# Eight of 22 k tiles of an FFN's last product computed as seven block products

## The chip, the cores and the metric

The kernel runs on one core of one Trainium2 chip. The metric is the device time of one execution in microseconds (us), the median of several runs; lower is better. The engines of the core are TensorE (PE, matrix products, with PEld for its weight loads), VectorE (DVE), ScalarE (ACT), GpSimd (POOL) and SyncE (SP). Operands lie in SBUF, matmul results in eight PSUM banks of 512 fp32 columns.

## What is computed

One block of a network for 512 tokens of width 1024, all in fp32: an FFN with half weight, a mixer (short convolution, gated linear attention, two gates), a second FFN with half weight, and a norm. The change concerns the second FFN and the end:

```python
def rmsnorm(x, g):
    y = x * lax.rsqrt(jnp.mean(x * x, axis=-1, keepdims=True) + EPS)
    return y * g

def swiglu(x, w_gu, w_down):
    g, u = jnp.split(x @ w_gu, 2, axis=-1)      # 1024 -> 2 x 2816
    return (jax.nn.silu(g) * u) @ w_down        # 2816 -> 1024

x = x + 0.5 * swiglu(rmsnorm(x, norm_ffn1_g), ffn1_w_gu, ffn1_w_down)
x = x + hybrid_mixer(rmsnorm(x, norm_mix_g), ...)
x = x + 0.5 * swiglu(rmsnorm(x, norm_ffn2_g), ffn2_w_gu, ffn2_w_down)
return rmsnorm(x, final_norm_g)
```

## The kernel before

**Three matmuls for one.** Each fp32 operand is split into a high part in the matmul's own type (fp32r) and a low part, the rest. A product is the sum of high x high, high x low and low x high. ScalarE casts the high part and VectorE subtracts to get the low part: for weights on lines 293 and 294 (`wh`, `wl`, rings of three buffers of 128 x 1024), for the FFN's hidden values on 649 and 650 (`split_hid`), for the operands of the sets below on 533 and 534 (`Operands.make`). The last two write to the pool `op`, 14 buffers of 128 x 1024.

**Weights.** `PLAN` lists the weight units in the order of their use and `STEPS` the steps that use them. `Weights.take` hands out the next split unit and issues the splits of the two steps after it. Raw units are loaded by SP (line 267) into the pool `f`, ten buffers, with 512 KB each. A down projection's unit is one k tile: 128 rows by 1024 columns.

**Sets.** Most of the up projections, and of the mixer's, are done in sets: a product of two by two blocks in seven block products instead of eight (Winograd's form). The names are m1, p2, q6, p5, q7, p4, p3. The weight sums of a set are made by accumulating DMAs on POOL (`Weights.add`, line 271) and one VectorE addition (`s3`, line 280); the operand sums by VectorE in place (`Operands.sum`); they are made once in each stage. A step of a set is 24 matmuls of 256 columns (line 485). `Operands.ORDER` is the order in which the operands are made; the steps themselves come in the order of `order()`.

**The FFN.** `ffn` computes a first group and two pairs of columns plainly (`plain_pair`), then nine sets (`up_set`), each of which leaves two k tiles of the hidden values. These are tiles of the pool `hid` (eleven buffers of 128 x 1024), which also holds the four normed operands at first. During the second FFN's sets `natural` transposes X so that tokens lie on partitions, X being the residual.

**The last product.** For the second FFN `last_down` follows: tokens on the partitions of the result, so the hidden values are the stationary operand and the weights the moving one. For each of 22 k tiles it runs four token tiles x two column halves x three matmuls of 512 columns (lines 700 to 702), into all eight PSUM banks. The last four k tiles (`TAIL`) are different: their weights and hidden values are split ahead, and bank by bank, token tile by token tile, the twelve matmuls that remain for a bank are followed by its evacuation into X (line 726), the final norm and the store, while TensorE goes on with the next bank.

**Who sets the order.** The framework's planner orders the instructions of each engine by its own simulation of the program, with program order as the priority, and places the waits; buffers of a pool are handed out in program order. Only the tail's part is in a fixed order (`manual_schedule`).

Of the kernel before, what the change touches and what calls it, by code (L numbers as in the profile page):

```python
# [12 lines left out]
ALU = mybir.AluOpType  # L13
ENG = mybir.EngineType

P = 128
S = 512
# [45 lines left out]
def full(mat, kt):  # L63
    return [(mat, k, 1, (0,), 1024) for k in range(kt)]
# [42 lines left out]
def units(us):  # L107
    for u in us:
        STEPS.append((len(PLAN), None))
        PLAN.append(u)  # L110
# [12 lines left out]
         ("conv", 3), ("cb", 0), ("cb", 1), ("r", 0), ("r", 1)]  # L123


def ffn_plan(up, down, plain, slow):

    units(group(up, KD, (0, DFF, P, DFF + P), slow))
    for f in range(2, plain):
        units(single(up, KD, f * P))  # L130
        units(single(up, KD, DFF + f * P))
    sets(up, [(s * HW, DFF + s * HW) for s in range(plain // 2, KF // 2)])
    units(full(down, KF))
    ENDS.append(len(STEPS))


# [31 lines left out]
def block_kernel(ctx: ExitStack, tc: tile.TileContext, xT, vecs, gf, gup, wgl, wts, out):  # L168
# [28 lines left out]
    def MM():  # L197
        cnt[0] += 1
        return ps.tile([P, S], F32, tag="mm", name=f"mm{cnt[0]}")
# [27 lines left out]
    class Weights:  # L227
# [3 lines left out]
        def __init__(self, ahead):  # L231
            self.ahead = ahead
            self.issued = 0
            self.taken = 0
            self.end = 0
            self.ready = []
            self.raw = {}
            self.loads = {}
            self.sums = {}

        def phase(self, early, first=6):


            self.early = early
            lo, self.end = self.end, [e for e in ENDS if e > self.end][0]
            for i in range(lo, self.end):
                n, p = STEPS[i]
                if p == "m1":
                    self.loads.setdefault(max(lo, i - first), []).append(n)
                    first = 6  # L250
                    self.sums.setdefault(max(lo + 3, i - 3), []).append(n)
            self.fetch(lo)

        def fetch(self, at):
# [15 lines left out]
        def add(self, out_, a):  # L270
            nc.gpsimd.dma_start(out_, a, accum_op=ALU.add)  # L271

        def issue(self):
            at = self.issued
            self.fetch(at)
            for n in self.loads.get(at, ()):
                self.raw[n] = [self.dma(n + i) for i in range(4)] + [tile_of("f", [P, 1024])]
            for n in self.sums.get(at, ()):
                a11, a12, a21, a22, s3 = self.raw[n]
                nc.vector.tensor_tensor(out=s3, in0=a11, in1=a21, op=ALU.add)  # L280
                self.add(a21, a22)
            n, p = STEPS[at]
            w = unit_cols(PLAN[n])
            if p is None:
                raw = self.raw[n]
            else:
                a11, a12, a21, a22, s3 = self.raw[n]
# [5 lines left out]
            nc.scalar.copy(h[:, :w], raw[:, :w])  # L293
            nc.vector.tensor_tensor(out=l[:, :w], in0=raw[:, :w], in1=h[:, :w].bitcast(F32),  # L294
                                    op=ALU.subtract)
# [162 lines left out]
    def mul(out_, a, b, eng=None):  # L458
        (eng or nc.vector).tensor_tensor(out=out_, in0=a, in1=b, op=ALU.mult)
# [34 lines left out]
    class Operands:  # L494

        ORDER = ("m1", "p2", "p5", "q6", "q7", "p4", "p3")

        def __init__(self, b):  # L500
            self.b = b
# [57 lines left out]
    def ffn(up, down, norm, nxt, plain, at):  # L559
# [6 lines left out]

        o = mm_group(up, KD, (0, DFF, P, DFF + P), xh, xl, extra=finish, slow=nxt is not None)
        row = rows[0]
        xn = {}

        def normed(j, l):

            if (j, l) not in xn:
                t = slice(l * HW, (l + 1) * HW)
                v = tile_of("hid", [P, 1024]).rearrange("p (k t) -> p k t", t=HW)
                for i in range(4):
                    k = 4 * j + i
# [8 lines left out]
        hid = []  # L586

        def plain_pair(f, g, u):
            if f % 2 == 0:
                hid.append(tile_of("hid", [P, 2, S]))  # L590
# [4 lines left out]
            mul(hid[-1][:, f % 2], s, t)  # L595

        xo.make("m1")
        plain_pair(0, o[0], o[1])
# [9 lines left out]
            plain_pair(f, g, u)  # L608

        def up_set(i):  # L610
            h = tile_of("hid", [P, 2, S])
            hid.append(h)

            def done(s, p):
                bank, v = s.bank, s.v
# [29 lines left out]
        def split_hid(k):  # L645

            h, l = (tile_of("op", [P, 2, S], F32R) for _ in range(2))
            t = hid[k // 2]
            nc.scalar.copy(h, t)  # L649
            nc.vector.tensor_tensor(out=l, in0=t, in1=h.bitcast(F32), op=ALU.subtract)  # L650
            return h, l

        us = full(down, KF)
        if nxt is None:
            return last_down(us, split_hid)
        o = [AUX(), AUX()] + [MM() for _ in range(KD - 2)]

        def mm(d, k, w, hl):
# [28 lines left out]
    def last_down(us, split_hid):  # L687
        X = XS[-1]
        gr = []
        for e in range(2):  # L690
# [6 lines left out]
        def mm(t, e, k, w, hl):  # L697
            wh, wl = (a[:, 512 * e : 512 * (e + 1)] for a in w)
            a, b = (v[:, k % 2, t * P : (t + 1) * P] for v in hl)
            nc.tensor.matmul(o[t][e], a, wh, start=k == 0, stop=False)  # L700
            nc.tensor.matmul(o[t][e], a, wl, start=False, stop=False)  # L701
            nc.tensor.matmul(o[t][e], b, wh, start=False, stop=k == KF - 1)  # L702

        for k in range(KF - TAIL):
            if k % 2 == 0:
                hl = split_hid(k)
            w = W.take(us[k])
            for t in range(NTB):
                for e in range(2):
                    mm(t, e, k, w, hl)  # L710
        w = [W.take(u) for u in us[KF - TAIL :]]
        hl = [split_hid(k) for k in range(KF - TAIL, KF, 2)]
        fin = []
        ys = [[] for _ in range(NTB)]

        def blocks(t):
            return t.rearrange("p (d i) -> p d i", i=P)

        last = NTB - 1

# [606 lines left out]
```

## Time and profile before

| | us |
|---|---|
| median of 3 runs | 1212.69 (1212.53 to 1212.84) |
| profiled execution, its own time | 1210.31 |
| span in the profile | 1208.6 |
| PE busy | 1196.6 |
| VectorE busy | 768.5 |
| ScalarE busy | 579.5 |
| granted clock of TensorE, mean | 0.999 |

The second FFN's last product begins at 1081.8 us of the span; its last matmul starts at 1201.3. A row of a timeline gives the start, the duration, the engine, the line, the operation, output and inputs, and in brackets how long the engine had been idle and what ended that. A row of groups gives engine, line, operation, shapes and count, then busy us and mean ns of one, then the idle time ahead of them. Matmuls overlap, so their durations are longer than their spacing.

### The profile page before, as it was taken

The numbers are of one execution on the slowest core, as the hardware profiler recorded it, in microseconds if no ns is written. First come the engines' busy times: TensorE is split into PE (matmuls) and PEld (weight loads), VectorE is DVE, ScalarE is ACT, GpSimd is POOL, SyncE is SP. The second block draws the span as 40 slices with busy tenths as digits, with TensorE's granted clock in tenths as the row PEclk, the third lists the DMA queues.
The fourth block names the chain that finished last, engine by engine and source line by source line (L and its number), as shares of the span: only waits on it lengthen the run. The fifth ranks groups of instructions, "written<-read, shape, count | busy, mean of one in ns | idle before, by whom it ended". The sixth has DMA issues, their size and how long they took to land.

```text
span 1208.6 us, 18730 instructions
## 1 busy us (share of the span) xinstructions
PE 1196.6 (99%) x7738; PEld 1095.3 (91%) x7738; DVE 768.5 (64%) x923; ACT 579.5 (48%) x718; POOL 89.7 (7%) x125
## 2 busy tenths in 40 slices
PE   9999999999999999998999999999999999999997
PEld 8899999988888889998999998888889999998886
DVE  7976666732277765767678685555597656583325
ACT  6554455532254466858554572234356445562323
POOL 0011111000010000010111100100001111100000
PEclk9999999999999999999999999999999999999999
DMA  9477777521162326766767766513347777752201
GB/s 348 98 197 188 179 190 180 174 88 61 53 244 88 89 69 159 205 170 165 186 184 175 191 178 214 200 63 129 113 101 192 186 176 176 182 182 90 70 1 69
DMA packets 55876, 181.33 MB, mean 150 GB/s; under 512 B 6288, under 2 KB 10512, under 8 KB 55792
## 3 DMA queue, kind: packets, MB, share of 16 engines
q1 hardware_dynamic: 36912, 124.27, 29.6%
q0 software_dynamic: 14240, 51.39, 23.0%
q10 hardware_dynamic: 4640, 4.49, 1.1%
q8 instruction: 60, 0.98, 0.3%
q14 instruction: 24, 0.20, 0.0%
HBM read 124.55 MB, written 8.39 MB: 110 GB/s over the span
## 4 chain that ended last, share of the span: by engine, by line
PE 97%; ACT 1%; DVE 1%; issue 0%; DMA 0%; DVEq 0%
PE mm L485 49%; PE mm L322 7%; PE mm L321 7%; PE mm L323 7%; PE mm L345 7%; PE mm L701 2%; PE mm L700 2%; PE mm L702 2%; PE mm L362 1%; PE mm L364 1%; PE mm L363 1%; PE aux L322 1%; PE aux L701 1%; PE aux L321 1%; PE aux L702 1%; PE aux L700 1%
## 5 line engine op out<-in xcount | busy, mean ns | idle before, releaser
L485 PE MATMUL mm<-op,wh 128*128 128x256 f32 x3360 | 608.0, 284 | 0.5 <-ACT wh L293 0.5
L293 ACT CAST wh<-f 128x1024 fp32r<-128x1024 f32 (+1 forms) x307 | 320.6, 1046 | 522.1 <-PE mm L485 205.6
L294 DVE TENSOR_TENSOR wl<-f,wh 128x1024 fp32r<-128x1024 f32 (+1 forms) x307 | 373.4, 1219 | 274.1 <-ACT wh L293 263.3
L485 PEld LDWEIGHTS mm<-op,wh 128*128 128x128 f32 x3360 | 523.8, 191 | 1.6 <-ACT wh L293 0.7
L485 PE MATMUL mm<-op,wl 128*128 128x256 f32 x1680 | 476.6, 284 | 2.5 <-DVE wl L294 2.5
L485 PEld LDWEIGHTS mm<-op,wl 128*128 128x128 f32 x1680 | 321.4, 191 | 2.8 <-DVE wl L294 2.7
L321 PE MATMUL mm<-op,wh 128*128 128x512 f32 x388 | 151.5, 390 | 0.0
L323 PE MATMUL mm<-op,wl 128*128 128x512 f32 x388 | 151.3, 390 | 0.0
L322 PE MATMUL mm<-op,wh 128*128 128x512 f32 x388 | 151.1, 389 | 0.0
L271 POOL DMA_DIRECT2D f<-f x90 | 77.7, 863 | 781.5 <-DVE wl L294 458.9
L323 PEld LDWEIGHTS mm<-op,wl 128*128 128x128 f32 x388 | 72.9, 188 | 15.1
L321 PEld LDWEIGHTS mm<-op,wh 128*128 128x128 f32 x388 | 72.9, 188 | 15.1
L322 PEld LDWEIGHTS mm<-op,wh 128*128 128x128 f32 x388 | 72.9, 188 | 14.9
L345 PE MATMUL mm<-op,wh 128*128 128x512 f32 x256 | 63.5, 390 | 0.2 <-DVE op L396 0.2
L345 PEld LDWEIGHTS mm<-op,wh 128*128 128x128 f32 x256 | 48.0, 188 | 10.5 <-issue 0.3
L490 ACT COPY tp<-mm 128x512 f32<-128x512 f32 x90 | 52.1, 579 | 2.8 <-PE mm L485 2.7
L700 PE MATMUL mm<-wh,op 128*128 128x512 f32 x108 | 42.1, 390 | 0.0
L701 PE MATMUL mm<-wl,op 128*128 128x512 f32 x108 | 42.1, 390 | 0.0
L702 PE MATMUL mm<-wh,op 128*128 128x512 f32 x108 | 42.1, 389 | 0.0
L650 DVE TENSOR_TENSOR op<-hid,op 128x1024 fp32r<-128x1024 f32 x22 | 26.9, 1222 | 17.7 <-ACT op L649 17.7
L280 DVE TENSOR_TENSOR f<-f,f 128x1024 f32<-128x1024 f32 x30 | 36.7, 1224 | 0.8
L345 PE MATMUL mm<-op,wl 128*128 128x512 f32 x128 | 34.3, 390 | 0.0
(247 smaller groups left out, 1113.8 us busy)
## 6 DMA issues: line engine op xcount, KB each, us to landing
f<-wts SPq DMA_DIRECT2D x219, 512.0 KB, 4.1
f<-f POOLq DMA_DIRECT2D x90, 512.0 KB, 4.9
X<-xT SPq DMA_DIRECT2D x8, 256.0 KB, 5.0
xs<-X POOLq DMA_DIRECT2D x8, 256.0 KB, 5.8
ga<-tp ACTq DMA_DIRECT2D x8, 256.0 KB, 2.8
gb<-tp ACTq DMA_DIRECT2D x8, 256.0 KB, 3.9
tp<-ga SPq DMA_DIRECT2D x8, 256.0 KB, 5.9
tp<-gb SPq DMA_DIRECT2D x8, 256.0 KB, 2.6
```

Source lines behind the costliest of these rows:

```text
L271: nc.gpsimd.dma_start(out_, a, accum_op=ALU.add)
L293: nc.scalar.copy(h[:, :w], raw[:, :w])
L294: nc.vector.tensor_tensor(out=l[:, :w], in0=raw[:, :w], in1=h[:, :w].bitcast(F32), op=ALU.subtract)
L321: nc.tensor.matmul(o, wh, ah, start=first, stop=False)
L322: nc.tensor.matmul(o, wh, al, start=False, stop=False)
L323: nc.tensor.matmul(o, wl, ah, start=False, stop=last)
L345: nc.tensor.matmul(o[c], w[:, s : s + P], a[k], start=k == 0 and j == 0, stop=k == kt - 1 and j == 2)
L485: nc.tensor.matmul(to, ww[:, s], aa[:, t], start=fresh and k == 0 and e == 0 and j == 0, stop=k == 3 and j == 2, skip_group_check=True)
L490: nc.scalar.copy(v, o)
L700: nc.tensor.matmul(o[t][e], a, wh, start=k == 0, stop=False)
L701: nc.tensor.matmul(o[t][e], a, wl, start=False, stop=False)
L702: nc.tensor.matmul(o[t][e], b, wh, start=False, stop=k == KF - 1)
```

## The change

- In the last product, the k tiles 8 to 17 come first, as before, each with 24 matmuls into eight banks. They are then closed and added to X with the factor 0.5 (eight VectorE instructions).
- The k tiles 0 to 7 follow as one two-by-two block product: two halves of four k tiles, two halves of 256 tokens, two halves of 512 columns, in seven block products in the order m1, p2, q6, p5, q7, p3, p4. Each takes two weight units (half of its k tiles each) of 128 x 1024 and runs 24 matmuls of 512 columns into two banks. Bank pair b collects m1, q6, q7 and p4, c collects p5 and p3, a holds p2. After each block product the running sum of its bank pair is added to one quarter of X with the factor 0.5 or -0.5, in two VectorE instructions (`uses`).
- The seven operands come from the hidden values through the class `Operands`; six of them are made during the ten direct k tiles, p4 after them. The weight sums are made as for the sets, for two sets of four units at once (`CHUNK_STEP`, `loads`, `sums`).
- The last four k tiles are as before, in new PSUM buffers; their raw weights are loaded at given steps (`pre`).
- The hidden values lie in one tile of 22 k tiles in both FFNs, and the normed operands in its last eight. The pools change: `f` eleven instead of ten, `tp` (scratch) eight instead of nine, `hid` one.
- `Operands.ORDER` has p3 ahead of p4, for all users of the class.

```diff
+CHUNK = 8
+CHUNK_ORDER = ("m1", "p2", "q6", "p5", "q7", "p3", "p4")
+CHUNK_STEP = {}
+
+def last_plan(down):
+    us = full(down, KF)
+    units(us[CHUNK : KF - TAIL])
+    firsts = []
+    for s in range(2):
+        firsts.append(len(PLAN))
+        PLAN.extend((down, 4 * j + 2 * s, 2, (512 * i,), 512) for i in range(2) for j in range(2))
+    CHUNK_STEP.update({(s, p): len(STEPS) + 2 * i + s for i, p in enumerate(CHUNK_ORDER)
+                       for s in range(2)})
+    STEPS.extend((n, p) for p in CHUNK_ORDER for n in firsts)
+    units(us[KF - TAIL :])
...
-    units(full(down, KF))
+    if slow:
+        units(full(down, KF))
+    else:
+        last_plan(down)
...
-                if p == "m1":
+                if p == "m1" and i in CHUNK_STEP.values():
+                    at = CHUNK_STEP[0, "m1"]
+                    self.loads.setdefault(at - (4 if i == at else 2), []).append(n)
+                    self.sums.setdefault(i, []).append(n)
+                elif p == "m1":
...
+            if self.end == len(STEPS):
+                c = CHUNK_STEP
+                for i, at in enumerate((c[0, "q6"], c[1, "q6"], c[1, "p3"], c[1, "p3"])):
+                    self.pre.setdefault(at, []).append(STEPS[self.end - TAIL + i][0])
...
-                self.raw[n] = [self.dma(n + i) for i in range(4)] + [tile_of("f", [P, 1024])]
+                self.raw[n] = [self.dma(n + i) for i in range(4)]
             for n in self.sums.get(at, ()):
+                self.raw[n].append(tile_of("f", [P, 1024]))
...
+            for n in self.pre.get(at, ()):
+                self.raw[n] = self.dma(n)
...
-        ORDER = ("m1", "p2", "p5", "q6", "q7", "p4", "p3")
+        ORDER = ("m1", "p2", "p5", "q6", "q7", "p3", "p4")
...
+        hid = tile_of("hid", [P, KF, S])
...
-                v = tile_of("hid", [P, 1024]).rearrange("p (k t) -> p k t", t=HW)
+                f = KF - KD + 4 * j
+                v = hid[:, f : f + 4, t]
...
-            h = tile_of("hid", [P, 2, S])
-            hid.append(h)
+            h = hid[:, plain + 2 * i : plain + 2 * i + 2]
...
-            nc.tensor.matmul(o[t][e], a, wh, start=k == 0, stop=False)
+            nc.tensor.matmul(o[t][e], a, wh, start=k in (CHUNK, KF - TAIL), stop=False)
             nc.tensor.matmul(o[t][e], a, wl, start=False, stop=False)
-            nc.tensor.matmul(o[t][e], b, wh, start=False, stop=k == KF - 1)
-
-        for k in range(KF - TAIL):
-            if k % 2 == 0:
-                hl = split_hid(k)
+            nc.tensor.matmul(o[t][e], b, wh, start=False, stop=k in (KF - TAIL - 1, KF - 1))
...
+        def add(t, e, bank, by):
+            xt = X[:, 4 * e : 4 * e + 4, t * P : (t + 1) * P]
+            nc.vector.scalar_tensor_tensor(out=xt, in0=blocks(bank), scalar=by, in1=xt,
+                                           op0=ALU.mult, op1=ALU.add)
+
+        ho = Operands(lambda j, l: hid[:, 4 * j : 4 * j + 4, l * HW : (l + 1) * HW])
+        hls = {k: split_hid(k) for k in (CHUNK, CHUNK + 2)}
+        more = [4, 6, 8, "m1", "p2", "p5", "q6", "q7", "p3"]
+        for k in range(CHUNK, KF - TAIL):
             w = W.take(us[k])
             for t in range(NTB):
                 for e in range(2):
-                    mm(t, e, k, w, hl)
+                    mm(t, e, k, w, hls[k - k % 2])
+            if more:
+                n = more.pop(0)
+                if isinstance(n, int):
+                    hls[CHUNK + n] = split_hid(CHUNK + n)
+                else:
+                    ho.make(n)
+        for t in range(NTB):
+            for e in range(2):
+                add(t, e, o[t][e], 0.5)
+        ho.make("p4")
+
+        uses = {"m1": [(0, 0, 0.5)], "p2": [(0, 0, 0.5)], "q6": [(1, 0, 0.5)],
+                "p5": [(1, 1, -0.5)], "q7": [(1, 1, -0.5)], "p3": [(1, 0, 0.5)],
+                "p4": [(0, 1, -0.5)]}
+        banks = {}
+        for p in CHUNK_ORDER:
+            b = {"p2": "a", "p5": "c", "p3": "c"}.get(p, "b")
+            fresh = b not in banks
+            if fresh:
+                banks[b] = [MM(), MM()]
+            bh, bl = ho.get(p)
+            for s in range(2):
+                h, l = W.take()
+                for i in range(2):
+                    k = 2 * s + i
+                    wh, wl = (a[:, 512 * i : 512 * (i + 1)] for a in (h, l))
+                    for e in range(2):
+                        c = slice(k * HW + e * P, k * HW + (e + 1) * P)
+                        to = banks[b][e]
+                        for n, (aa, ww) in enumerate(((bh, wh), (bh, wl), (bl, wh))):
+                            nc.tensor.matmul(to, aa[:, c], ww,
+                                             start=fresh and k == 0 and n == 0,
+                                             stop=k == 3 and n == 2, skip_group_check=True)
+            for l, e, by in uses[p]:
+                for t in range(2):
+                    add(2 * l + t, e, banks[b][t], by)
+        o[:] = [[MM(), MM()] for t in range(NTB - 1)] + [[AUX(), AUX()]]
         w = [W.take(u) for u in us[KF - TAIL :]]
         hl = [split_hid(k) for k in range(KF - TAIL, KF, 2)]
...
-    FFN = dict(f=10, hid=11, tp=9)
+    FFN = dict(f=11, hid=1, tp=8)
```

More of the change, by code (lines that the diff above doesn't have):

```diff
@@ L239, in __init__ @@
             self.sums = {}
+            self.pre = {}
         def phase(self, early, first=6):
@@ L286, in issue @@
             else:
-                a11, a12, a21, a22, s3 = self.raw[n]
+                a11, a12, a21, a22, s3 = (self.raw[n] + [None])[:5]
                 raw = {"m1": a11, "p2": a12, "q6": a11, "p5": a21, "q7": s3, "p4": a22,
@@ L585, in ffn @@
         xo = Operands(normed)
-        hid = []
         def plain_pair(f, g, u):
-            if f % 2 == 0:
-                hid.append(tile_of("hid", [P, 2, S]))
             s, t = T(), T()
@@ L594, in plain_pair @@
             mul(t, u, row)
-            mul(hid[-1][:, f % 2], s, t)
+            mul(hid[:, f], s, t)
         xo.make("m1")
@@ L647, in split_hid @@
             h, l = (tile_of("op", [P, 2, S], F32R) for _ in range(2))
-            t = hid[k // 2]
+            t = hid[:, k : k + 2]
             nc.scalar.copy(h, t)
@@ L654, in ffn @@
         if nxt is None:
-            return last_down(us, split_hid)
+            return last_down(us, hid, split_hid)
         o = [AUX(), AUX()] + [MM() for _ in range(KD - 2)]
@@ L685, in natural, with last_down @@
         nc.scalar.copy(X[:, i], o)
-    def last_down(us, split_hid):
+    def last_down(us, hid, split_hid):
         X = XS[-1]
@@ L699, in mm, with blocks @@
             a, b = (v[:, k % 2, t * P : (t + 1) * P] for v in hl)
-            nc.tensor.matmul(o[t][e], a, wh, start=k == 0, stop=False)
+            nc.tensor.matmul(o[t][e], a, wh, start=k in (CHUNK, KF - TAIL), stop=False)
             nc.tensor.matmul(o[t][e], a, wl, start=False, stop=False)
-            nc.tensor.matmul(o[t][e], b, wh, start=False, stop=k == KF - 1)
-        for k in range(KF - TAIL):
-            if k % 2 == 0:
-                hl = split_hid(k)
+            nc.tensor.matmul(o[t][e], b, wh, start=False, stop=k in (KF - TAIL - 1, KF - 1))
+        def blocks(t):
+            return t.rearrange("p (d i) -> p d i", i=P)
+        def add(t, e, bank, by):
[6 more added lines that the diff above has]
+        for k in range(CHUNK, KF - TAIL):
             w = W.take(us[k])
```

2 lines of the change are left out of this document (removed).

## The prediction

> **What bounds the kernel.** First the page: the busy line of TensorE and the chain that ended last.
>
> ```profile
> span 1208.6 us, 18730 instructions
> ...
> PE 1196.6 (99%) x7738; PEld 1095.3 (91%) x7738; DVE 768.5 (64%) x923; ACT 579.5 (48%) x718; POOL 89.7 (7%) x125
> ...
> PE 97%; ACT 1%; DVE 1%; issue 0%; DMA 0%; DVEq 0%
> ```
>
> TensorE is busy in 1196.6 of 1208.6 us, and 97% of the chain is its own queue. A busy PE can still hold short waits, so next the waits of PE, longest first, in the stretch from 480 to 560 us, the mixer's first sets:
>
> ```profile
> PE mm L485 <- DVE wl L294: 2.5, 1, 2.5
> PE aux L957 <- DVE qk L459: 0.8, 1, 0.8
> PE mm L485 <- ACT wh L293: 0.5, 1, 0.5
> ```
>
> Over the whole span PE has only two others, at the kernel's start (1.1 and 0.2 us in the same view); neither FFN has any after that. The rest is matmuls in a row, so a matmul less is worth one spacing, as long as its operands are made in time. Third, the stretches that the change touches, by engine (us, then busy PE, PEld, DVE, ACT, POOL):
>
> ```profile
> 896.90:923.00 26.10, 26.10 (x219) 26.06 (x219) 23.76 (x24) 16.81 (x21) 3.72 (x5) 1.00 0.82 193
> 1070.00:1081.60 11.60, 11.60 (x99) 11.60 (x98) 10.82 (x11) 9.16 (x11) 0.86 (x1) 1.00 0.74 207
> 1087.00:1136.00 49.00, 49.00 (x218) 40.59 (x217) 15.57 (x13) 13.27 (x13) 0.00 (x0) 1.00 0.30 102
> 1202.00:1208.60 6.60, 0.00 (x0) 0.00 (x0) 2.48 (x8) 1.74 (x4) 0.00 (x0) 0.81 0.37 142
> ```
>
> They are the second FFN's first set, the end of its sets, the middle of its last product, and what follows the last matmul. In the last product VectorE works 15.57 of 49 us, so there is room for more preparation; in the two set stretches it works 91 to 93% of the time, and TensorE still never stops.
>
> **Spacing of the matmuls.** A piece of the chain in the sets (256 columns), and from the timeline the first matmul of the last product, two L700 matmuls exactly one k tile (24 matmuls) apart, and the last matmul.
>
> ```profile
> 897.12 25.91 PE mm L485 x216
> ```
>
> ```profile
> 1081.84 0.40 PE L700 MATMUL mm<-wh,op 128*128 128x512 f32 x1
> ...
> 1172.99 0.39 PE L700 MATMUL aux<-wh,op 128*128 128x512 f32 x1
> ...
> 1178.43 0.39 PE L700 MATMUL aux<-wh,op 128*128 128x512 f32 x1
> ...
> 1201.32 0.39 PE L702 MATMUL aux<-op,op 128*128 128x512 f32 x1
> ```
>
> A k tile takes 1178.43 - 1172.99 = 5.44 us, a 512-column matmul 5.44 / 24 = 0.2267 us; the 0.39 us in the rows is latency, of which the next matmuls hide the rest. Check: 528 matmuls from 1081.84 to 1201.32 (the last start) are 527 x 0.2267 = 119.5 us, as the rows have it. In the sets 256 columns take 25.91 / 216 = 0.12 us, or 0.24 us per 512.
>
> **Part 1, the matmuls.** Eight k tiles cost 8 x 24 = 192 matmuls. Seven products of 256 tokens by 512 columns by four k tiles cost 7 x (4 x 2 x 3) = 168 of the same 512-column form (operand stationary, weights moving). Removed: 24 x 0.2267 = 5.44 us, all on the path. The last product becomes 10 x 5.44 + 14 half products x 2.72 + 4 x 5.44 = 114.2 us instead of 119.7.
>
> [...]
>
> **Part 2, preparing weights and operands.** From the groups of the last 170 us VectorE's two costliest and ScalarE's first (busy us, mean ns of one), then the accumulating DMAs with their median landing, then three VectorE instructions in a row:
>
> ```profile
> L294 DVE TENSOR_TENSOR wl<-f,wh 128x1024 fp32r<-128x1024 f32 x31 | 37.9, 1223 | 42.6 <-ACT wh L293 42.6
> L650 DVE TENSOR_TENSOR op<-hid,op 128x1024 fp32r<-128x1024 f32 x11 | 13.5, 1224 | 16.8 <-ACT op L649 16.8
> ```
>
> ```profile
> L293 ACT CAST wh<-f 128x1024 fp32r<-128x1024 f32 x30 | 31.5, 1050 | 52.8 <-PE aux L702 34.0 <-PE mm L485 9.9 <-issue 7.0
> ```
>
> ```profile
> f<-f POOLq DMA_DIRECT2D x90, 512.0 KB, 4.9
> ```
>
> ```profile
> 1076.12 1.23 DVE L294 TENSOR_TENSOR wl<-f,wh 128x1024 fp32r<-128x1024 f32 x1
> 1077.26 0.68 DVE L618 TENSOR_TENSOR tp<-mm,tp 128x512 f32<-128x512 f32 x1
> 1077.86 1.22 DVE L294 TENSOR_TENSOR wl<-f,wh 128x1024 fp32r<-128x1024 f32 x1
> ```
>
> Back to back a 1024-element instruction of VectorE takes 1.14 us of its queue and a 512-element one 0.60. Added in the last product: six more weight splits (14 half units for 8 units), three more operand splits net (seven for four), four in-place sums for them, two sums s3, and 14 + 8 evacuations ahead of the tail's: 15 x 1.14 + 22 x 0.60 = 30.3 us of VectorE, and 9 x 1.05 = 9.5 us of ScalarE. None of it is on the path if it fits. The tightest stretch is the seven products, 38.1 us, with the direct k tile ahead of them, 5.4. At most it holds 14 weight splits, four tail splits, two operand splits, the sum and split for p4 (22 x 1.14 = 25.1) and 22 evacuations (13.2): 38.3 of 43.5 us, 88%. The other operands and s3 lie in the ten direct k tiles, where two thirds of VectorE is free. At 93% in the stretch from 1070 TensorE had no wait, so 88% costs nothing. Without that cover each late instruction would cost its 1.14 us.
>
> Weights for a half product follow the same ring of three wh/wl as now: a split may begin when the step three back has ended, two steps (5.44 us) before it is wanted, and takes 1.05 + 1.22 us. The sets do the same at 8 x 3 x 0.12 = 2.88 us per step; here it is 2.72. Nothing.
>
> **Part 3, accumulating DMAs.** Six are added, in chains (a22 into a21, a21 into a11, a11 into a12), 4.9 us each. The one that is wanted first is a21 into a11, by q6. It can go when m1's split of its half is done, and q6's split lies four steps later: in the ring of three that is, for the second half, one direct k tile and three half products, 5.44 + 3 x 2.72 = 13.6 us, less 2.3 for m1's own split; against it stand 4.9, or 9.8 if both halves' stand in POOL's queue one behind the other. Nothing by these rows; the bound is one landing, 4.9 us, once, if POOL has its four in the worst order. The loads move earlier on SP, past nothing but each other, and the f ring has one buffer more.
>
> **Part 4, the junction with the tail.** The tail's first accumulators are new PSUM buffers. If they fall on the banks of the last product (p4), its evacuation comes between. From the timeline, the last matmul of a group and the VectorE instruction it releases:
>
> ```profile
> 1182.28 0.39 PE L702 MATMUL mm<-op,op 128*128 128x512 f32 x1
> ...
> 1182.71 0.69 DVE L726 SCALAR_TENSOR_TENSOR X<-mm,X 128x512 f32<-128x512 f32 x1 [11.52 <-PE mm L702]
> ```
>
> 0.43 us from the matmul's start, then 0.69. The first of p4's two banks ends four spacings (0.91 us) before the tail would start, so its evacuation ends 0.43 + 0.69 - 0.91 = 0.2 us after that; with a release to PE at most 0.3. On other banks it is 0. I take 0.2. The 6.6 us behind the last matmul stay.
>
> **Part 5, the order p3 before p4 and the pools.** The operand order holds for both FFNs and the mixer, and there p4 is wanted first. In the second FFN the first set begins at 897.1, 24 matmuls or 2.88 us a step (the chain's piece above); the pair of operand splits in it is one row of the timeline:
>
> ```profile
> 911.53 2.36 DVE L534 TENSOR_TENSOR op<-hid,op 128x1024 fp32r<-128x1024 f32 x2
> ```
>
> p4 is the seventh step: 897.1 + 6 x 2.88 = 914.4. Its split is now the first of the pair, done at 912.7; as the second it is done at 913.9. 0.5 us remain, so I take nothing; the bound is one split, 1.14 us, in each of three stages, 3.4 us, or as much gained where the mixer's 3.8 us of waits shift. One scratch buffer fewer (8 of 9) is still a whole set of six ahead: nothing, within the same bound.
>
> **Sum.** The profiled execution took 1210.31 us, its span 1208.6; -5.44 + 0.2 = -5.24 makes 1205.1. On the median of the runs, 1212.69, it is 1207.45; I say 1207.5. About 0.2%, 2.4 us, is what can be told from no change: faster is below 1210.3, slower above 1215.1.
>
> **Rivals.**
>
> *One tile, whole-tile waits (slower).* All of the hidden operand now lies in one tile. If a read of one slice waited for writes to the others, the last product of either FFN would begin only after the sets' last write:
>
> ```profile
> 1084.72 0.69 DVE L459 TENSOR_TENSOR hid<-tp,tp 128x512 f32<-128x512 f32 x1
> ```
>
> 1085.4 + 1.05 for the cast is 1086.5, against 1081.84: 4.6 us, and up to 5.5 with the low part, in each of two FFNs: 1207.5 + 9.2 to 11 = 1216.7 to 1218.5. It decides as soon as that write is the first operand's releaser. Against it, X is one tile as well (its loads, its first reader; durations in ns, then first and last start):
>
> ```profile
> L1269 SPq DMA_DIRECT2D X<-xT x8: 420/432/574, 1.2 to 5.7; - x8
> ```
>
> ```profile
> L405 ACT ACTIVATE acc<-X x3: 617/617/632, 4.3 to 832.1; 128x512 f32<-128x512 f32 x3
> ```
>
> Its first slice is read at 4.3 us while loads of others are still being issued. [...]
>
> *Splits behind the last product.* If VectorE has the four tail splits and two operand splits queued behind p4's evacuations, the tail waits about 0.8 + 6 x 1.14 = 7.7 us: 1207.3 + 7.7 = 1215.0. Only the last pair must wait for a product (p3's buffers), and it has p4's 5.44 us for 1.05 + 1.22.
>
> *A cheaper matmul saved.* If the block form runs at the sets' 0.24 us, 168 x 0.0133 = 2.2 us are lost: 1209.7. For it: two banks in turn instead of eight. Against: operand and width are those of L700. [...]
>
> *Order and pools cost.* Part 5's bounds, one to three splits and some of the mixer: 1208.6 to 1212. VectorE at 91% speaks for it, the 0.5 us against. The same shuffle can also gain: 1203.7 to 1206.5.
>
> *The change does not save matmuls*: then x7738 stays; 168 + 10 x 24 + 96 = 504 against 528 in the code says otherwise, and I give it nothing.
>
> **Chances.** Forecast 0.62 (its own range 1206.9 to 1208.5); cheaper matmul 0.08; order and pools cost 0.15, of which 0.07 still below 1210.3; they gain 0.05; splits behind the last product 0.03; whole tile 0.07. Faster 0.62 + 0.08 + 0.07 + 0.05 = 0.82, same 0.08 + 0.03 = 0.11, slower 0.07. The range 1206.0 to 1210.8 leaves out the last two, a part of the costs and most of the gain, about 0.18.
>
> **What would show it.** Right: 7714 matmuls, the block's matmuls 0.2267 us apart, no new wait of PE in the last product but 0.2 to 0.3 us at the tail's start, 6.6 us behind the last matmul, the mixer's waits as now. Wrong: a PE wait on wl or op between the products, on X or hid at the start of either last product, on f by an accumulating DMA, or a first set that stops at p4.

## The result, and the profile after

The changed kernel takes 1215.2 us (median of 10 runs, 1213.92 to 1217.1) against 1212.61 of the kernel before beside it. The ratio is 1.0023, with a 95% interval from 1.0014 to 1.0032: slower, by 2.6 us, where 5.2 us faster was forecast. The profiled execution took 1214.66 us, its span 1212.7.

The page first: the span, the busy line, and the mean clock that TensorE was granted.

```profile
span 1212.7 us, 18791 instructions
...
PE 1196.8 (99%) x7714; PEld 1094.0 (90%) x7714; DVE 802.4 (66%) x960; ACT 588.8 (49%) x727; POOL 95.5 (8%) x131
```

```profile
core 0: 1212.7 us, clock 0.995
```

There are 24 matmuls fewer, x7714 against x7738, and yet PE's busy time is not lower. What the change was to do in the last product, it did. From the chain of waits (start, us, what), the seven block products in one piece, and from the timeline the first matmul of the last product, the change from its last block product to its tail, and the last matmul:

```profile
1146.03 38.08 PE mm L785 x168
```

```profile
1091.44 0.40 PE L734 MATMUL mm<-wh,op 128*128 128x512 f32 x1
...
1183.72 0.39 PE L785 MATMUL mm<-wh,op 128*128 128x512 f32 x1
1183.94 0.39 PE L734 MATMUL mm<-op,op 128*128 128x512 f32 x1
...
1205.48 0.39 PE L736 MATMUL aux<-op,op 128*128 128x512 f32 x1
```

38.08 / 168 = 0.2267 us each; from the first start to the last it is 1205.48 - 1091.44 = 114.04 us, against 1201.32 - 1081.84 = 119.48 before. The 5.44 us are there to the hundredth. But the last product begins 9.6 us later. Of these, 2.0 us lie in the profile ahead of the mixer's end (its last matmul starts at 852.72 before and 854.73 after; the last section takes up a part of them); the rest arises at the boundary between the mixer and the second FFN. The waits of PE over the whole span (engine, line, waited for: us in total, times, longest) hold three that the kernel before did not have: the first, and the last two. The one on L910 is in the mixer and is worth 0.3 us; the other two stand at the boundary:

```profile
PE aux L464 <- ACT tp L407: 3.6, 1, 3.6
PE mm L520 <- DVE wl L329: 2.5, 1, 2.5
PE aux L235 <- POOL ones L232: 1.1, 1, 1.1
PE aux L1035 <- DVE qk L494: 0.8, 1, 0.8
PE mm L520 <- ACT wh L328: 0.5, 1, 0.5
PE aux L925 <- DVE g L910: 0.3, 1, 0.3
PE mm L380 <- ACT wh L328: 0.3, 1, 0.3
```

L464 is a row sum of the norm that closes the mixer, L380 here the second FFN's first group. Neither was touched by the change. The same 16 us of both kernels by engine (us, busy and instructions of PE, PEld, DVE, ACT, POOL, then granted clock, DMA share, GB/s), first before, then after:

```profile
850.00:866.00 16.00, 16.00 (x72) 13.28 (x71) 8.56 (x10) 4.92 (x6) 0.89 (x1) 1.00 0.42 115
```

```profile
850.00:866.00 16.00, 12.15 (x43) 8.86 (x42) 9.81 (x18) 7.44 (x10) 0.00 (x0) 0.79 0.83 321
```

PE starts 43 matmuls instead of 72, the clock falls to 0.79, and the DMA share doubles. The timeline of PE after shows the order in which this happens, and two stretches of SP's timeline the loads, with nothing between them:

```profile
854.73 0.39 PE L358 MATMUL mm<-op,wl 128*128 128x512 f32 x1
858.69 0.80 PE L464 MATMUL aux<-tp,ones_r 128*128 128x512 f32 x1 [3.57 <-ACT tp L407]
859.42 0.80 PE L465 MATMUL aux<-tp,ones_r 128*128 128x512 f32 x1
860.01 2.13 PE L718 MATMUL aux<-ident,X 128*128 128x128 f32 x8
862.42 3.45 PE L380 MATMUL mm<-op,wh 128*128 128x512 f32 x8 [0.27 <-ACT wh L328]
```

```profile
792.46 0.33 SPq L299 DMA_DIRECT2D f<-wts  x1
```

```profile
847.14 2.36 SPq L299 DMA_DIRECT2D f<-wts  x5
```

In the kernel before, the row sum comes inside the group, with no wait (its timeline):

```profile
868.36 1.08 PE L345 MATMUL mm<-op,wl 128*128 128x512 f32 x4
869.27 0.39 PE L429 MATMUL aux<-tp,ones_r 128*128 128x512 f32 x1
```

So two things differ at this boundary. The row sums and two of the groups of four transposes (L718) now stand ahead of the first group on PE, and PE waits for the norm. And SP issues nothing for 54 us. Its own waits from 790 to 850 us name the releaser, first before, then after:

```profile
SPq L267 <- DVE wl L294: 59.7, 8, 21.4
```

```profile
SPq L299 <- DVE acc L444: 54.3, 1, 54.3
SPq L299 <- DVE wl L329: 5.0, 1, 5.0
```

L444 adds the square of a tile of X, held in a scratch tile of the pool `tp`, to the norm's sum. The addresses in the two built programs tell why a weight load should wait for that. `f` begins at byte 121952 of each partition with 4096 bytes a buffer; ten buffers end at 162912. In the mixer's phase `f` has ten, and the pool behind it is `tp`: its first two tiles lie at 162912 to 167008. The FFN phases of the changed kernel give `f` an eleventh buffer, and it lies at exactly these bytes. The new `f` pool hands out its first buffer and then its last one, so the second FFN's second load gets it: its wait in the program is on the L444 instruction that reads the last tile there, and nine loads stand behind it on SP.

### The profile page after: what moved, and what is told of

Same layout as the page of the kernel before. It is cut to its first block, busy times and chain, and to the rows that moved or that the text cites. A ratio compares the mean times of both kernels' runs of the same rounds, so it can differ in the third digit from the quotient of the medians.

```text
span 1212.7 us, 18791 instructions
## 1 busy us (share of the span) xinstructions
PE 1196.8 (99%) x7714; PEld 1094.0 (90%) x7714; DVE 802.4 (66%) x960; ACT 588.8 (49%) x727; POOL 95.5 (8%) x131
## 4 chain that ended last, share of the span: by engine, by line
PE 98%; DVE 1%; ACT 1%; issue 0%; POOL 0%; DVEq 0%; POOLq 0%
PE mm L520 49%; PE mm L357 7%; PE mm L358 7%; PE mm L356 7%; PE mm L380 7%; PE mm L785 3%; PE mm L736 2%; PE mm L734 2%; PE mm L735 2%; PE mm L397 1%; PE mm L398 1%; PE mm L399 1%; PE aux L357 1%; PE aux L358 1%; PE aux L356 1%; PE aux L1076 1%
## 5 line engine op out<-in xcount | busy, mean ns | idle before, releaser
L328 ACT CAST wh<-f 128x1024 fp32r<-128x1024 f32 (+1 forms) x313 | 326.6, 1046 | 505.1 <-PE mm L520 205.8
L329 DVE TENSOR_TENSOR wl<-f,wh 128x1024 fp32r<-128x1024 f32 (+1 forms) x313 | 380.5, 1219 | 234.7 <-ACT wh L328 229.2
L520 PEld LDWEIGHTS mm<-op,wl 128*128 128x128 f32 x1680 | 322.6, 192 | 3.1 <-DVE wl L329 3.0
L303 POOL DMA_DIRECT2D f<-f x96 | 83.0, 865 | 856.2 <-DVE wl L329 425.7
L358 PEld LDWEIGHTS mm<-op,wl 128*128 128x128 f32 x388 | 72.8, 188 | 15.0
L380 PE MATMUL mm<-op,wh 128*128 128x512 f32 x256 | 64.9, 396 | 0.3 <-ACT wh L328 0.3
L380 PEld LDWEIGHTS mm<-op,wh 128*128 128x128 f32 x256 | 48.9, 192 | 11.3 <-ACT wh L328 0.7
L568 ACT CAST op<-hid 128x1024 fp32r<-128x1024 f32 x21 | 22.1, 1050 | 30.0 <-PE aux L735 20.7
L785 PE MATMUL mm<-wh,op 128*128 128x512 f32 x112 | 34.6, 389 | 0.0
L380 PE MATMUL mm<-op,wl 128*128 128x512 f32 x128 | 34.3, 389 | 0.0
L380 PEld LDWEIGHTS mm<-op,wl 128*128 128x128 f32 x128 | 24.0, 188 | 5.1
```

The source lines that it names most:

```text
L358: nc.tensor.matmul(o, wl, ah, start=False, stop=last)
L380: nc.tensor.matmul(o[c], w[:, s : s + P], a[k], start=k == 0 and j == 0, stop=k == kt - 1 and j == 2)
L520: nc.tensor.matmul(to, ww[:, s], aa[:, t], start=fresh and k == 0 and e == 0 and j == 0, stop=k == 3 and j == 2, skip_group_check=True)
L785: nc.tensor.matmul(to, aa[:, c], ww, start=fresh and k == 0 and n == 0, stop=k == 3 and n == 2, skip_group_check=True)
```

## Experiments

Theory A: this place of the eleventh `f` buffer costs the 7.8 us by which the result misses the forecast. Its rivals: the order of p3 and p4, the single hidden tile or the smaller scratch pool moved the planner's order (B), or it is the number of `f` buffers and not their place (C). Within A, the late loads themselves or the changed order of instructions may carry the price.

**First run: ten buffers in the last phase.**

```diff
-    with phase("small3", **FFN):
+    with phase("small3", f=10, hid=1, tp=8):
```

> The changed kernel, with ten f buffers instead of eleven in the last phase alone (the second FFN); everything else is as changed. Theory A (place): the eleventh buffer of f lies over two scratch tiles of the mixer that its closing norm still uses, the second load of the second FFN gets this buffer and waits for the norm, and ten loads queue behind it on SP; without the buffer the first loads go out near 812 us again as in the kernel before, TensorE has no wait at the start of the second FFN, and the time is 1207.4 us (1206.7 to 1208.2): the 7.8 us that the boundary cost are gone and the 5.2 that the blocks save are left. Theory B (order of instructions): the eight scratch tiles, the whole hid tile or the new order of p3 and p4 made the planner put the row statistics ahead of the FFN's matmuls; f's count changes nothing of that, and the time stays at 1215 (1214 to 1216).

Measured: 1208.14 us (1207.9 to 1208.27), ratio to before 0.9963 (0.9951 to 0.9976). SP's waits from 790 to 850 us are those of before again, and the 16 us are full:

```profile
SPq L299 <- DVE wl L329: 56.7, 7, 21.4
```

```profile
850.00:866.00 16.00, 16.00 (x72) 13.27 (x71) 9.41 (x11) 6.07 (x8) 0.89 (x1) 1.00 0.31 103
```

Everything that B names was left in (the order of p3 and p4, the single hidden tile, eight scratch tiles), so B falls.

**Second run: the buffer in the kernel before.** One scratch tile is given up as well, as in the changed kernel; the first run had eight scratch tiles too and no stall, so the tile is not what costs.

```diff
-    with phase("small3", **FFN):
+    with phase("small3", f=11, hid=11, tp=8):
```

> The kernel before, with eleven f buffers and eight scratch tiles instead of ten and nine in the last phase alone; the last product is the old one. Theory A: the loads of the second FFN wait for the mixer's closing norm here too, and the whole price stands alone: 1220.3 us (1219.5 to 1221), with about 3.9 us of waits of TensorE at the start of the second FFN and half clock behind them. Theory B: nothing, 1212.6 (1212 to 1213.2), as the instructions of the last product are what changed.

Measured: 1220.55 us (1219.44 to 1222.9) against 1212.69, ratio 1.007 (1.0056 to 1.0083). PE's waits, longest first, and the stretch:

```profile
PE aux L429 <- ACT tp L372: 3.6, 1, 3.6
PE mm L485 <- DVE wl L294: 2.5, 1, 2.5
```

```profile
850.00:866.00 16.00, 12.15 (x43) 8.88 (x42) 9.40 (x17) 7.44 (x10) 0.00 (x0) 0.79 0.79 305
```

The old last product with one `f` buffer more has the whole stall, down to the 43 matmuls. The price by itself is 1220.55 - 1212.69 = 7.9 us.

**Third run: eleven buffers, another tenant below.**

```diff
-    with phase("small2", f=10, tp=6, v=4, qk=2, g=1, y=4, small=1):
+    with phase("small2", f=10, v=4, tp=6, qk=2, g=1, y=4, small=1):
```

> The changed kernel with eleven f buffers throughout, but with the mixer's pools laid out in another order: the pool v, whose tiles are read for the last time long before the mixer's end, lies right behind f, and the scratch tiles behind v. The eleventh f buffer of the second FFN now lies over v. Theory A (place, not count): the loads go out early and the time is 1207.4 us (1206.5 to 1208.5). Theory C (count: eleven buffers let loads run further ahead and collide with the mixer's transfers, or the planner fills the longer ring in another order): 1214 to 1216, as in the changed kernel. The mixer's own instructions may shift a little with its pools, for up to 0.5 us either way.

Measured: 1206.58 us (1205.67 to 1207.55), ratio 0.9951 (0.9938 to 0.9963), no wait at the boundary. Eleven buffers cost nothing over tiles that are read for the last time early: place, not number; C falls. This is the best of the versions, faster than both kernels.

**Fourth run: the old order of p3 and p4 on top of the first run.**

```diff
-        ORDER = ("m1", "p2", "p5", "q6", "q7", "p3", "p4")
+        ORDER = ("m1", "p2", "p5", "q6", "q7", "p4", "p3")
```

> As the first run (ten f buffers in the last phase), and besides the old order of the set's products in both FFNs, p4 ahead of p3. Theory A has no part in this edit: 1207.4 us, within 0.5 of the first run. If the new order of p3 and p4 costs or saves something of its own, the difference between this run and the first shows it; up to 0.9 us could lie in the first FFN and at its end, where the changed kernel's mixer starts 0.85 us later than before.

Measured: 1207.81 us (1206.59 to 1209.89), 0.3 below the first run and inside its own spread of 3.3 us: the order of the operands is worth nothing that can be seen here.

**Fifth run: TensorE kept busy through the wait.** Sixteen matmuls into the row sum's bank ahead of it, on an operand that is ready (`fill` is the closing norm's sixth k tile).

```diff
-            return rstd_rows([self.acc], D)[0]
-
-    def rstd_rows(accs, width):
+            return rstd_rows([self.acc], D, self.h[KD - 3] if self.goff == V_G2 else None)[0]
+
+    def rstd_rows(accs, width, fill=None):
...
-            st = AUX()
+            st = AUX(); [nc.tensor.matmul(st, ones_r, fill, start=True, stop=True) for _ in range(16 if fill is not None else 0)]
             nc.tensor.matmul(st, ones_r, h, start=True, stop=False)
```

> The changed kernel, with 16 matmuls more of 512 columns whose sums nothing reads, put between the mixer's last product and the closing norm's row sums: they fill the 3.6 us in which TensorE waited there. What the boundary costs falls into two parts: the group's first matmul at 862.4 instead of 855 us (it waits for a cast on ScalarE that ends then, whatever TensorE does meanwhile), and half clock to about 865.9. Theory A1 (both count): the half clock behind the wait goes and 1.7 us are saved, 1213.4 (1212.8 to 1214.2). Theory A2 (the clock is most of the price): 1211 or below. Theory A3: the 1.7 us that TensorE still waits between the transposes and the group's first matmul bring the half clock back: 1215.

Measured: 1213.72 us (1212.06 to 1214.92; 11 runs), ratio to before 1.0011 (1.0002 to 1.002). The stretch that ran at 0.71 and 0.58 in the changed kernel now runs at full clock (first the changed kernel, then this run):

```profile
856.00:862.00 6.00, 3.31 (x10) 2.07 (x10) 3.40 (x8) 3.81 (x6) 0.00 (x0) 0.71 0.98 399
862.00:866.00 4.00, 3.73 (x11) 2.87 (x11) 3.93 (x7) 2.26 (x3) 0.00 (x0) 0.58 0.31 117
```

```profile
856.00:862.00 6.00, 5.19 (x25) 3.81 (x23) 3.48 (x6) 3.15 (x4) 0.00 (x0) 1.00 1.01 414
862.00:866.00 4.00, 3.27 (x15) 2.58 (x16) 3.58 (x9) 3.06 (x4) 0.00 (x0) 1.00 0.37 117
```

About 1.5 us of the price are the clock's (1215.2 - 1213.72). The intervals of the two ratios overlap, so the medians alone do not settle it; the profiles agree with it, 358.0 us from the mixer's last matmul to the end in the changed kernel and 356.3 here. The larger part stays: the group still starts 7.4 us after the mixer's last matmul (863.38 against 855.98 in this run's timeline), whatever TensorE does meanwhile.

**Sixth run: early loads, the changed kernel's order.** The load that gets the bad buffer goes to GpSimd's queue.

```diff
-            lo, self.end = self.end, [e for e in ENDS if e > self.end][0]
+            lo, self.end = self.end, [e for e in ENDS if e > self.end][0]; self.nth = 0
...
-            nc.sync.dma_start(t[:, :w], wts[o : o + P * w].rearrange("(p n) -> p n", p=P))
+            self.nth += 1; (nc.gpsimd if self.end == len(STEPS) and self.nth == 2 else nc.sync).dma_start(t[:, :w], wts[o : o + P * w].rearrange("(p n) -> p n", p=P))
```

> The changed kernel with all its eleven f buffers, but the one load that gets the buffer over the scratch tiles (the second load of the second FFN) goes out on GpSimd's queue instead of SP's; GpSimd has no other work there until the first set. The other ten loads then no longer queue behind its wait and land before 830 us. The instructions of TensorE and ScalarE stand in the same order as in the changed kernel: row sums and transposes ahead of the group, the casts of its weights behind the norm's. Theory A-loads (the late landing itself is what costs): the group's first matmuls could start near 857, the time falls to 1207.4 to 1209. Theory A-order (the late loads cost because the planner saw them and put the norm's work ahead, so that TensorE waits for the row sums in any case): nothing is won although the data are there: 1215 (1214 to 1215.8), the wait of 3.6 us stands.

Measured: 1215.55 us (1213.83 to 1216.19; 11 runs), ratio 1.002 (1.0011 to 1.0029): nothing won. The wait moved to GpSimd (its waits from 700 to 900 us), SP's other loads went out from 813.84 us (its timeline up to 830 us), the last of them at 844 us, and the DMA share at the boundary was 0.14, but PE stood as before (its waits, and ScalarE's timeline):

```profile
POOL f L299 <- DVE acc L444: 77.0, 1, 77.0
```

```profile
813.84 16.45 SPq L299 DMA_DIRECT2D f<-wts  x7
```

```profile
850.00:866.00 16.00, 11.76 (x41) 8.55 (x41) 10.07 (x19) 7.44 (x10) 0.00 (x0) 0.80 0.14 43
```

```profile
PE aux L464 <- ACT tp L407: 3.6, 1, 3.6
...
PE mm L380 <- ACT wh L328: 0.3, 1, 0.3
```

```profile
857.65 0.62 ACT L407 CAST tp<-acc 128x512 fp32r<-128x512 f32 x1 [0.90 <-DVE acc L444]
858.28 1.28 ACT L485 ACT_TABLE_LOAD   x1
860.54 0.21 ACT L485 ACTIVATE st_s<-st_v 128x16 f32<-128x16 f32 x1 [0.97 <-DVE st_v L468]
860.66 2.92 ACT L328 CAST wh<-f 128x1024 fp32r<-128x1024 f32 x3
```

Three of the first group's four weight units had gone out by 816 us, some 45 us before its first matmul at 861.74, and the fourth, GpSimd's, at 847.40; the time is the same. In the built programs TensorE's instructions, and ScalarE's, stand in the same order as in the changed kernel. The first casts of the group's weights (L328) stand behind the norm's square root in ScalarE's fixed order, and the row sums stand ahead of the group on PE. The order is what costs, not the landing.

**Ninth run, its counterpart: late loads, the other order.** The second FFN's first group in program order on TensorE and ScalarE.

```diff
-        o = mm_group(up, KD, (0, DFF, P, DFF + P), xh, xl, extra=finish, slow=nxt is not None)
+        with (tc.manual_schedule(engines={ENG.PE, ENG.Activation}) if nxt is None else ExitStack()): o = mm_group(up, KD, (0, DFF, P, DFF + P), xh, xl, extra=finish, slow=nxt is not None)
```

> The changed kernel with its eleven f buffers and its late loads, but the second FFN's first group is issued in program order on TensorE and ScalarE (row sums after the sixth k tile, as in the kernel before), so the planner can't put the norm's row sums ahead of it. It is the counterpart of the sixth run, which had early loads and the planner's order. If the order carries the price: the loads go out near 847 us and land near 852, the group's first weights are cast on ScalarE behind the norm's last square (about 856.5) and are there near 857.5; TensorE waits 2.6 us instead of 7.4 and, with or without half clock for some us behind it, the time is 1210.0 to 1211.7. If the late landing by itself carries it, the group can't run earlier than it did: 1214 to 1216. If neither: 1207.4.

Measured: 1212.18 us (1209.94 to 1216.21; 11 runs), ratio 1.0 (0.9989 to 1.0011); the profiled execution 1211.36. SP still waits 54.3 us for L444. PE's longest wait, its timeline from the mixer's last matmul to the first row sum, and ScalarE's at the first casts:

```profile
PE mm L380 <- ACT wh L328: 3.0, 1, 3.0
```

```profile
855.61 0.39 PE L358 MATMUL mm<-op,wl 128*128 128x512 f32 x1
858.99 2.11 PE L380 MATMUL mm<-op,wh 128*128 128x512 f32 x8 [2.99 <-ACT wh L328]
...
874.54 1.08 PE L380 MATMUL mm<-op,wl 128*128 128x512 f32 x4
875.46 0.39 PE L464 MATMUL aux<-tp,ones_r 128*128 128x512 f32 x1
```

```profile
857.39 0.61 ACT L443 ACTIVATE tp<-X 128x512 f32<-128x512 f32 x1
857.91 2.94 ACT L328 CAST wh<-f 128x1024 fp32r<-128x1024 f32 x3
```

The group starts 3.4 us after the mixer instead of 7.7, with the loads as late as ever. What is left of the wait is ScalarE's order again: the first casts stand directly behind the norm's last square (L443), while in the first run three of them come ahead of it (847.26, 850.64 and 856.08 us, the square at 857.66). The interval of the ratio, 0.9989 to 1.0011, does not reach that of the changed kernel, 1.0014 to 1.0032. The median is 0.5 us above the range expected for the order. The runs spread over 6.3 us, more than in any other kernel here, and the spread goes with the clock: the mean granted clock falls from 0.998 in the fastest run to 0.993 in the slowest, and 0.005 of 1210 us are 6 us. Where in the kernel the slower ones lose it is not shown, since only one run was profiled.

**Seventh and eighth run: what the pools' order is worth by itself.** The kernel before with eleven `f` buffers and the third run's pools; and the third run's kernel with ten `f` buffers in the last phase.

```diff
-    FFN = dict(f=10, hid=11, tp=9)
+    FFN = dict(f=11, hid=11, tp=8)
...
-    with phase("small2", f=10, tp=6, v=4, qk=2, g=1, y=4, small=1):
+    with phase("small2", f=10, v=4, tp=6, qk=2, g=1, y=4, small=1):
```

> The kernel before with its old last product, with eleven f buffers and eight scratch tiles in both FFNs as the changed kernel has them, and with the mixer's pools in the other order (v behind f, the scratch tiles behind v) as in the third run. Theory A: no boundary wait, so the time is that of the kernel before but for what the pools' order does in the mixer: 1212.6, or 1211.1 if the third run's 1.5 us over the first are the pools' doing. The third run less this one is then the last product with its blocks by itself: 5.2 to 5.5 us. Rival: the third run's lead comes from elsewhere and the blocks save less (under 4) or more (over 6.5).

Measured: 1212.72 us (1212.04 to 1215.66), ratio 1.0003 (0.9995 to 1.0012): the pools' order and the eleventh buffer, once it lies elsewhere, are worth nothing in the kernel before. The third run less this one, 1206.58 - 1212.72 = -6.1 (5.2 to 5.5 us faster was expected), and the eighth less this one, -5.5, are the new last product with its hidden tile and its operand order.

```diff
-    with phase("small2", f=10, tp=6, v=4, qk=2, g=1, y=4, small=1):
+    with phase("small2", f=10, v=4, tp=6, qk=2, g=1, y=4, small=1):
...
-    with phase("small3", **FFN):
+    with phase("small3", f=10, hid=1, tp=8):
```

> The third run's kernel (mixer's pools in the other order) with ten f buffers in the last phase, as in the first run. It separates the 1.5 us between the first and the third run: 1206.6 (1205.8 to 1207.3) if the pools' order in the mixer gives them, 1208.1 if the eleventh buffer does. A third reading is that both are the same and that the half clock behind the 2.5 us wait at the mixer's start, which the first run's profile shows (granted clock 0.89 from 540 to 570 us) and the third's doesn't (1.00), falls on some executions only: then this run spreads over 1205.7 to 1208.3.

Measured: 1207.25 us (1206.92 to 1207.8), between the first and the third run. What separates the four versions without the stall (1208.14, 1206.58, 1207.81, 1207.25) is not settled; their mean is 1207.4. In the profiles all of it lies ahead of the mixer's last matmul (next table), in the order of the clock granted from 540 to 570 us: 1.00 in the third run, 0.94 in the fourth and eighth, 0.89 in the first.

All eleven kernels side by side, from the timelines: the start of the mixer's last matmul, that of the group's first, the gap, and the span behind the group's first matmul.

| kernel | last of mixer | first of group | gap | from there to the end |
|---|---|---|---|---|
| before | 852.7 | 852.9 | 0.2 | 355.7 |
| seventh run | 854.7 | 854.9 | 0.2 | 355.7 |
| second run | 855.4 | 863.1 | 7.7 | 355.7 |
| changed | 854.7 | 862.4 | 7.7 | 350.3 |
| first run | 855.8 | 856.1 | 0.2 | 350.1 |
| third run | 853.6 | 853.8 | 0.2 | 350.2 |
| fourth run | 855.5 | 855.7 | 0.2 | 350.2 |
| eighth run | 855.2 | 855.4 | 0.2 | 350.2 |
| fifth run | 856.0 | 863.4 | 7.4 | 348.9 |
| sixth run | 854.4 | 861.7 | 7.4 | 351.3 |
| ninth run | 855.6 | 859.0 | 3.4 | 350.4 |

Two independent steps: the last column says blocks or not (355.7 or about 350.2), the gap says what the boundary did. In the runs with the gap of 7.4 to 7.7 us, 1.3 us of row sums and transposes lie in the gap instead of behind it, and the lower clock adds to the last column: nothing in the fifth run (348.9; 1.00 granted from 862 to 866 us), 1.4 us in the changed kernel (0.58, and 1.00 from 866 to 870), 2.4 in the sixth run (0.50, and 0.94 from 866 to 870).

## Why the prediction was wrong

**The step that failed** is in part 3: "the f ring has one buffer more", a term that was put at nothing without a price. The sizes of the pools were looked at as numbers only: is a ring with one more or one fewer still deep enough? Where the extra buffer lies was not asked, nor which stage's tile it takes over; it lies over the closing norm's scratch tiles and costs 7.9 us (second run). The opening part's view of where PE waits ended at "neither FFN has any after that"; the start of the second FFN was taken as untouched since none of its lines is in the diff. The ending on the slower side was given 0.07, to whole-tile waits at the last products, which did not come: no PE wait after 862.5 us. The rival "order and pools cost", at 0.15, named the pools, but its price came from part 5, one to three VectorE splits and at most 1212 us, and not from a buffer's place.

**The price, term by term,** against the first run: the gap grew from 0.23 to 862.42 - 854.73 = 7.69, so 7.5 us; the group's 96 matmuls took 23.42 us in the chain instead of 96 x 0.2267 = 21.8, so 1.7 for the lower clock (0.58 granted from 862 to 866 us); given back are the two row sums (0.45) and the two groups of transposes (0.44 each), which now lie in the gap. 7.5 + 1.7 - 0.45 - 0.9 = 7.8, against 7.9 measured by the second run (and 7.6 between these two profiles, from the mixer's last matmul to the end). With the forecast's own sum, 7.8 - 5.24 = +2.6: the changed kernel's 1215.2 against 1212.6.

**How the buffer does it.** Shown: with the buffer over the scratch tiles the stall is there (second run) and without it, or with it over other tiles, not (first, third); early loads under the same order win nothing (sixth); a better order under the same late loads wins 3.0 us of median and 4.3 of the gap (ninth). So the price is paid for the order of TensorE and ScalarE and not for the landing of the loads: SP's 54 us are a sign. The planner, which orders the engines by its own simulation, put the norm ahead of the group once the second load had to wait for the norm; that this wait is its reason is argued from the runs with and without it, its simulation was not looked into. Why it held back the first unit's cast too, whose load left SP at 792.46 us, is not shown by any run.

**Right, with its reason.** Part 1: x7714, 0.2267 us each, 119.48 to 114.04. Part 2: VectorE was to fit in the products at up to 88%, and it is 31.52 of 38.10 us, 83%, with no wait of PE:

```profile
1146.00:1184.10 38.10, 38.10 (x170) 31.55 (x169) 31.52 (x35) 20.93 (x22) 1.72 (x2) 1.00 0.32 77
```

Part 4: 0.2 us were taken for the junction; it is one spacing, 1183.94 - 1183.72 = 0.22, so nothing. Part 5's first half, the order of p3 and p4: nothing (fourth run; and from the group's start to the last product it is 228.9 us in the kernel before and in the first run alike, 1081.84 - 852.94 and 1084.96 - 856.06). One scratch tile fewer: nothing (first and seventh run). The forecast, 1207.5, is about the time of the kernel without the accident: the four versions without it lie from 1206.58 to 1208.14. That their mean, 1207.4, meets it to 0.1 us is luck, as they differ by more among themselves for reasons that are not settled.

## What to carry to other kernels

A pool that grows in one phase lies over some tile of the phase before it: ask whose, who reads that tile last, and which of the new phase's loads gets the buffer; a change in one stage can be paid for at the start of another that it doesn't touch. When a stall shows late loads and a changed order together, do not take the loads for the cause: here early loads under the bad order won nothing of 7.9 us, and a better order under the same late loads won 3.0. A planner that orders by simulation can turn one late buffer into a static order that costs even when the data are early, so compare the order of the instructions around every boundary, not only around the edit.

## What the runs showed of the hardware

The clock behind a wait was not the same from profile to profile. Every one of these kernels has the same wait of 2.5 us on L329 (L294 in the old ones) early in the mixer; behind it the granted clock from 540 to 570 us is 1.00 in three profiles, 0.94 in five and 0.89 in three. Here the third run and the first:

```profile
556.00:560.00 4.00, 3.48 (x29) 3.48 (x30) 3.88 (x5) 3.95 (x5) 0.86 (x1) 1.00 0.27 80
560.00:564.00 4.00, 4.00 (x36) 4.00 (x35) 2.55 (x6) 3.85 (x8) 0.00 (x0) 1.00 1.00 168
```

```profile
556.00:560.00 4.00, 3.43 (x16) 3.43 (x17) 3.38 (x4) 3.95 (x5) 0.86 (x1) 0.50 0.24 76
560.00:564.00 4.00, 4.00 (x26) 4.00 (x26) 1.82 (x2) 1.68 (x3) 0.00 (x0) 0.70 1.01 184
```

Both leave that wait at 556.5 us. From 540 to 570 us the third run's TensorE does 213 matmuls and the first run's 194, and the mixer's last matmul comes at 853.6 and 855.8: about 2.2 us that no instruction explains. The kernel before was profiled without the drop (1.00 from 540 to 570 us), the changed one with a part of it (0.94), which is a part of why the profiles differ by 4.1 us in span and the medians by 2.6.

The length of the wait alone does not tell in these eleven profiles what clock follows. The 2.5 us in the mixer have the lower clock behind them in eight profiles and the full clock in three. At the boundary TensorE's longest wait is 3.6 us in the changed kernel, in the second run and in the sixth, and the mean clock from 850 to 866 us is 0.79, 0.79 and 0.80; in the ninth run it is 3.0 us, and the clock is 1.00, as it is in the fifth run, whose longest wait there is 0.8 us. What decides whether the clock falls is not shown by any run.
